# Row shifts of the v tiles: one transfer of 127 or 126 rows, or one of 112 rows and one of the rest

## The chip, the cores and the metric

The kernel runs on one core of one Trainium2 chip. The metric is the device time of one execution in microseconds (us); the figure for a kernel is the median of its timed runs. One further execution was recorded by the hardware profiler. Its record (the trace, and the page of summaries made from it) is where all durations below come from.

Engines are named as in the profile: PE is the matrix engine (PEld its weight loads), DVE the vector engine, ACT the scalar engine, POOL the general-purpose engine, SP the queue processor that issues nearly all transfers here. SPq, DVEq and the like are the sequencers of these engines.

## The reference, cut to what matters

One decoder layer on 256 tokens of width 2048, all in float32. One input projection gives q, k, v, two gate columns per head, a cross-attention query and a SiLU gate path; a gated delta rule works on q, k and v, a cross-attention into 256 memory tokens runs beside it, both are gated and one output projection adds to the residual.

The change touches the causal depthwise convolution that q, k and v pass before the delta rule. Of v there are 3072 columns, and each output row needs its own row and the three rows before it:

```
def causal_depthwise_conv(x, w):          # w has 4 taps
    # y[t, c] = x[t,c] w[3,c] + x[t-1,c] w[2,c] + x[t-2,c] w[1,c] + x[t-3,c] w[0,c]
qkv = silu(causal_depthwise_conv(p[..., :c_qkv], conv_w))
v = qkv[..., 2 * DN_QK_WIDTH:].reshape(B, S, DN_V_HEADS, DN_HEAD_DIM)
```

(The comment line spells out what the library call computes with four taps; rows before the first are zero.)

## The kernel before, in words

**The main stream.** The list `PLAN` (line 55 on) names the weight tiles in the order in which the matrix engine uses them: the memory's values and keys (V, K), the gate columns (ab), the cross-attention query (x), k, q, v and z columns of the input projection, then the output projection (o). One step is one weight tile of 128 x 1024 float32, 512 KB. SP loads it into a staging tile `st` (five buffers); ACT rounds it to the matmul's fp32r format (line 335, the high half of `wt`); DVE subtracts to get the low half (line 339); PE then multiplies high by high, high by low and low by high. `wt` has four buffers, and line 346 keeps two of them prepared ahead. So every weight tile needs a place in the in-order queues of SP, ACT and DVE, and whatever makes one of these engines wait holds up the next weight tile.

`proj_a` (line 355) is used for k and q: the output has the columns on the partitions and the 256 tokens along the free dimension. `proj_b` (line 394) is used for the rest: the output has 128 tokens on the partitions and 512 columns along the free dimension, and there are two such outputs, r = 0 and r = 1, for the two halves of the 256 tokens. The v columns are six proj_b tiles, g = 0 to 5 (`v0` to `v5` in `PLAN`), spread between k, q and z tiles.

**The side work.** Everything that is not the main stream is written as generators. A planned clock, `now[0]`, moves with the planned cost of each matmul; a generator that yields a number is resumed that many planned microseconds later, a plain `yield` resumes it when the operations that it has issued are planned to be over (plus 0.25). `Transfers.dma_start` (line 131, used as `sd`) plans 3.0 us for any transfer, however many it is followed by, and passes it to SP. `VLAND` (line 45) is 5.0, `CALM` 1.6: `calm()` lets a generator wait until DVE's planned queue is short. The program order that results is handed to a framework, which lays out each engine's queue and adds the semaphores.

**The convolution of v** (`v_done`, line 1158). The tokens lie on the partitions, so the value of an earlier token lies on another partition, and a transfer has to move it. For each r, `go()` does this: ACT copies the projection out of PSUM (`vs`); for r = 0 four transfers load the taps (`vw`); `shift(a, val, r, 1)` moves the values down by one row into `a`; five planned microseconds later DVE computes t = v w1 + a w0; `shift(b, two, r, 2)` moves that sum down by two rows into `b`, while DVE computes y = v w3 + a w2; five planned microseconds later DVE adds b. Silu and a scale follow, and with both r done, `delta(g)` (line 1224) does the delta rule for four heads.

`shift(dst, src, r, n)` (line 1162) is therefore called with n = 1 and n = 2 for each of the twelve (g, r). It issues one transfer of 128 - n rows of 2 KB from partitions 0 to 127 - n to partitions n to 127. What is missing at the top, n rows, comes from the last rows of the r = 0 tile when r is 1 (a transfer of n rows), and is zero when r is 0 (a memset on POOL). In the trace the tiles `a`, `b`, `t` and `y` are all called vc, so the shift by one is `vc<-vs` and the shift by two is `vc<-vc`; line 86 is the helper that records every pinned operation and transfer, line 103 the one for DVE, ACT and POOL.

**What else goes through SP around the v tiles.** Weight tiles (`st<-W_d`); rows of the cumulated gate broadcast to all partitions (`erow<-dgc`, line 717), from which ACT computes the decays (`dec`); blocks of the matrix to be inverted, written out and read back (`dN<-dec`, `inN<-dN`, `n<-dN`, `dY<-inXT`, `dX<-inN`, `Y<-dY`, `XN<-dX`, lines 921 to 993).

Of the kernel before, what the change touches and what calls it, by code (L numbers as in the profile page):

```python
# [72 lines left out]
def hybrid_kernel(ctx: ExitStack, tc: tile.TileContext, x, xT, memT, W, prm_d, cst_d, out):  # L73
# [61 lines left out]
    sd = Transfers()  # L135
# [9 lines left out]
    def S2(name, shape, dt=F32):  # L145
        return s2p.tile([128] + list(shape), dt, name=name, tag="s2")
# [26 lines left out]
    def give(pt, t):  # L173

        idle[held.pop(id(pt))[0]].append(t)
# [30 lines left out]
    def spawn(gen, delay=0.0):  # L206
        nproc[0] += 1
        heapq.heappush(heap, (now[0] + delay, nproc[0], gen))
# [21 lines left out]
    def until(cond):  # L230
        while not cond():
            yield POLL
# [14 lines left out]
    def calm(queued=CALM):  # L247

        while ve.end > now[0] + queued:
            yield ve.end - now[0] - queued  # L250
# [907 lines left out]
    def v_done(g):  # L1158

        raw, w, val, two = [None] * 2, [], [None] * 2, [None] * 2  # L1160

        def shift(dst, src, r, n):

            sd.dma_start(dst[n:128], src[r][0 : 128 - n])
            if r:
                sd.dma_start(dst[0:n], src[0][128 - n : 128])
            else:
                po.memset(dst[0:n], 0.0)

        def done(r, pt):  # L1170
            def go():
                yield 0.2
                v = val[r] = S2("vs", [512])
                se.copy(v, pt)
                give(pt, se.end)
                if r == 0:
                    for j in range(4):
                        w.append(S2("vw", [4, 128]))
                        sd.dma_start(w[j], dtap.rearrange("(t k) c -> k t c", k=4)[3 - j][4 * g : 4 * g + 4]
                                     .unsqueeze(0).to_broadcast([128, 4, 128]))  # L1180
                yield
                a, y, t = [S2("vc", [512]) for _ in range(3)]
                shift(a, val, r, 1)
                yield VLAND
                yield from calm()
                w3, w2, w1, w0 = [t_.rearrange("c t e -> c (t e)") for t_ in w]

                ve.tensor_tensor(out=t, in0=v, in1=w1, op=ALU.mult)
                ve.tensor_tensor(out=y, in0=a, in1=w0, op=ALU.mult)
                ve.tensor_tensor(out=t, in0=t, in1=y, op=ALU.add)  # L1190
                two[r] = t
                yield
                yield from until(lambda: two[0] is not None)
                b = S2("vc", [512])
                shift(b, two, r, 2)
                yield from calm()
                ve.tensor_tensor(out=y, in0=v, in1=w3, op=ALU.mult)
                ve.tensor_tensor(out=a, in0=a, in1=w2, op=ALU.mult)
                ve.tensor_tensor(out=y, in0=y, in1=a, op=ALU.add)
                yield VLAND  # L1200
                yield from calm()
                v = y
                ve.tensor_tensor(out=v, in0=y, in1=b, op=ALU.add)
                yield
                se.activation(v, v, AF.Silu)
                vv = v.rearrange("c (w e) -> c w e", w=4)
                yield from until(lambda: all(p in grams for p in (2 * g, 2 * g + 1)))
                for h in range(4):
                    se.activation(vv[:, h, :], vv[:, h, :], AF.Copy, scale=sV[:, r, 4 * g + h : 4 * g + h + 1])
                yield  # L1210
                raw[r] = vv
                ready.add(f"v{g}{r}")
                if r == 1:
                    vss[g] = raw
                    yield from delta(g)
            spawn(go())
        return done
# [271 lines left out]
```

## Time and profile before

| what | value |
|---|---|
| timed runs | 944.04, 945.95, 948.47 us; median 945.95 us |
| the profiled execution | 948.84 us, its span (first to last instruction) 947.1 us |
| PE busy | 868.1 us, 92% of the span |
| DVE busy | 620.4 us, 66% |
| ACT busy | 538.2 us, 57% |
| granted clock of PE, mean over the span | 0.955 |
| transferred | 181.58 MB, 192 GB/s on average |

The page also follows back the chain of work that ended last: at each step to what released it, or to the instruction before it on its engine. An entry "DMA vc<-vs" there is time between the issue of a shift by one and its landing, during which nothing else on that chain was going on; an entry "issue" is time in which an engine waited for something that the profile does not show. A view of waits gives, per engine, the idle time that ended when something else finished, how often, and the longest. A view of windows gives, for stretches of time, the busy time of each engine (with the number of instructions), the granted PE clock as a share of full speed, and the mean busy share of the 16 transfer engines. An engine's idle time costs something only where PE, which is busy nearly throughout, is idle too.

### The profile page before, as it was taken

What the parts mean: (1) busy time and instruction counts of PE and PEld (TensorE: products, weight loads), DVE (VectorE), ACT (ScalarE), POOL (GpSimd) and SP (SyncE); (2) the same over time, 40 slices, a digit from 0 to 9 for tenths busy, and PEclk for the clock granted to TensorE, in tenths of its full rate; (3) what the DMA queues carried; (4) which work ended last, traced back from release to release, by engine and by line L of the source; (5) the groups of instructions that cost most, each with busy time, mean ns of one, the idle gap of its engine ahead of it and who ended that gap; (6) DMA issues with size and microseconds to landing.
All of it is one profiled execution on the core that took longest, in us unless ns stands there. A gap on an engine that the chain in (4) does not pass through costs nothing.

```text
span 947.1 us, 13137 instructions
## 1 busy us (share of the span) xinstructions
PE 868.1 (92%) x4789; PEld 724.3 (76%) x4789; DVE 620.4 (66%) x1080; ACT 538.2 (57%) x927; POOL 44.0 (5%) x45
## 2 busy tenths in 40 slices
PE   8999999999999997967997996965949999999998
PEld 5888888888888876856885884754838888888886
DVE  6769886496799637937777984527558655544442
ACT  6656656887447557825954663645837564343341
POOL 1000000000000000111000001100001000000000
PEclk8999999999999997986998997997979999999999
DMA  9855465477778846646745873645545455856560
GB/s 352 280 186 189 146 217 157 134 211 213 216 246 254 248 133 214 206 156 183 221 141 165 270 214 112 211 134 192 164 126 170 141 178 164 279 190 214 198 214 31
DMA packets 144737, 181.58 MB, mean 192 GB/s; under 512 B 24256, under 2 KB 115256, under 8 KB 144672
## 3 DMA queue, kind: packets, MB, share of 16 engines
q1 hardware_dynamic: 144240, 180.47, 60.4%
q8 instruction: 37, 0.61, 0.3%
q10 hardware_dynamic: 432, 0.28, 0.1%
q14 instruction: 28, 0.23, 0.1%
HBM read 167.58 MB, written 6.89 MB: 184 GB/s over the span
## 4 chain that ended last, share of the span: by engine, by line
PE 76%; DMA 12%; ACT 4%; DVE 3%; issue 2%; SPq 1%; ACTq 0%; DVEq 0%
PE pb L86 63%; DMA vc<-vs 9%; PE pa L86 6%; DMA erow<-dgc 2%; SPq L86 1%; DVE wt L339 1%; PE pU L86 1%; PE pO L86 1%; ACT wt L335 1%; DVE vc L103 1%; PE pm L86 1%; ACT dec L103 1%; PE pyT L86 1%; PE pkq L86 1%; DMA mst<-memT_d 1%
## 5 line engine op out<-in xcount | busy, mean ns | idle before, releaser
L339 DVE TENSOR_TENSOR wt<-st,wt 128x1024 fp32r<-128x1024 f32 (+1 forms) x274 | 332.6, 1217 | 167.7 <-ACT wt L335 165.3
L335 ACT CAST wt<-st 128x1024 fp32r<-128x1024 f32 (+1 forms) x274 | 286.2, 1047 | 245.9 <-PE pb L86 191.7
L86 PE MATMUL pb<-wt,hkt 128*128 128x512 f32 x1536 | 372.0, 400 | 32.6 <-DVE wt L339 32.6
L86 PEld LDWEIGHTS pb<-wt,hkt 128*128 128x128 f32 x1536 | 292.5, 193 | 95.9 <-DVE wt L339 34.8
L86 PE MATMUL pb<-wt,yhi 128*128 128x512 f32 x512 | 158.0, 390 | 0.0
L86 PE MATMUL pa<-hkt,wt 128*128 128x512 f32 (+1 forms) x768 | 144.5, 345 | 8.0 <-ACT raw L103 7.7
L86 PEld LDWEIGHTS pa<-hkt,wt 128*128 128x128 f32 x768 | 119.9, 192 | 26.1 <-ACT raw L103 8.0
L86 PEld LDWEIGHTS pb<-wt,yhi 128*128 128x128 f32 x512 | 95.7, 188 | 19.6
L86 PE MATMUL pb<-wt,ylo 128*128 128x512 f32 x256 | 99.7, 389 | 0.0
L86 PE MATMUL pb<-wt,mkt 128*128 128x512 f32 x384 | 92.2, 400 | 2.7 <-DVE mkt L103 1.9
L86 PEld LDWEIGHTS pb<-wt,mkt 128*128 128x128 f32 x384 | 73.6, 193 | 20.1 <-issue 3.2
L103 DVE TENSOR_TENSOR vc<-vc,vw 128x512 f32<-128x512 f32 x24 | 16.5, 687 | 77.0 <-DMA vc<-vs 60.5
L86 PEld LDWEIGHTS pb<-wt,ylo 128*128 128x128 f32 x256 | 48.1, 188 | 10.1
L103 ACT ACT_TABLE_LOAD x31 | 39.8, 1283 | 4.1 <-DVE acc L103 3.6
L103 ACT ACTIVATE acc<-raw,prm 128x256 f32<-128x256 f32 x24 | 12.1, 505 | 46.1 <-DVE raw L103 46.1
L103 DVE SCALAR_TENSOR_TENSOR acc<-raw,prm,acc 128x255 f32<-128x255 f32 (+2 forms) x72 | 34.3, 477 | 2.5 <-ACT acc L103 2.1
L103 DVE TENSOR_TENSOR inT<-inXT,inN 96x1 f32<-96x1 f32 (+22 forms) x92 | 29.2, 343 | 3.3 <-DMA inN<-dN 2.5
L103 DVE TENSOR_REDUCE inXT<-inT 96x1 f32<-96x1 f32 (+22 forms) x92 | 28.6, 338 | 0.7
L86 PE MATMUL pO<-u,aT 128*128 128x128 f32 x96 | 13.7, 288 | 15.5 <-ACT u L103 15.5
L86 PEld LDWEIGHTS pO<-u,aT 128*128 128x128 f32 x96 | 12.8, 203 | 16.2 <-ACT u L103 15.9
L103 DVE TENSOR_TENSOR vc<-vc 128x512 f32<-128x512 f32 x36 | 24.6, 684 | 0.1
L103 ACT ACTIVATE dec<-erow,gcc 128x128 f32<-128x128 f32 x48 | 16.1, 392 | 13.8 <-DMA erow<-dgc 13.8
(202 smaller groups left out, 697.2 us busy)
## 6 DMA issues: line engine op xcount, KB each, us to landing
st<-W_d SPq DMA_DIRECT2D x272, 512.0 KB
erow<-dgc SPq DMA_DIRECT2D x24, 256.0 KB
vw<-dtap SPq DMA_DIRECT2D x24, 256.0 KB
dN<-dec SPq DMA_DIRECT2D x12, 256.0 KB
n<-dN SPq DMA_DIRECT2D x12, 256.0 KB
vc<-vs SPq DMA_DIRECT2D x12, 254.0 KB
vc<-vc SPq DMA_DIRECT2D x12, 252.0 KB
xraw<-xT_d SPq DMA_DIRECT2D x8, 256.0 KB
```

Source lines behind the costliest of these rows:

```text
L86: return lambda *a, **k: pin(getattr(self.eng, op)(*a, **k))
L103: return pin(getattr(self.eng, op)(*a, **k))
L335: pin(se.eng.copy(hi[:, w] if parts > 1 else hi, st[:, w] if parts > 1 else src))
L339: pin(ve.eng.tensor_tensor(out=lo[:, w] if parts > 1 else lo, in0=st[:, w] if parts > 1 else src, in1=hi[:, w] if parts > 1 else hi, op=AL ...
```

## The change

The transfer of 128 - n rows in `shift` becomes two: rows 0 to 111 (112 rows) go to partitions n to 111 + n, and the remaining 16 - n rows (15 for n = 1, 14 for n = 2) go to partitions 112 + n to 127. The same bytes land in the same places. The transfer or memset of the top n rows is untouched, and so are the pauses, the order in which the work is written down and everything else. Over the kernel, 24 transfers become 48.

```
         def shift(dst, src, r, n):
 
-            sd.dma_start(dst[n:128], src[r][0 : 128 - n])
+
+            sd.dma_start(dst[n : 112 + n], src[r][0:112])
+            sd.dma_start(dst[112 + n : 128], src[r][112 : 128 - n])
             if r:
                 sd.dma_start(dst[0:n], src[0][128 - n : 128])
             else:
```

## The prediction

> **What bounds the kernel now.** I read first where PE has idle time, in a table of three stretches of the span (length, then busy time and instruction count of PE, PEld, DVE, ACT, POOL, then PE clock, transfer share, GB/s):
>
> ```profile
> 0.00:340.00 340.00, 335.77 (x1883) 278.90 (x1884) 257.14 (x484) 217.18 (x347) 17.32 (x23) 0.99 0.69 217
> 340.00:720.00 380.00, 309.07 (x1853) 258.93 (x1852) 245.93 (x455) 220.35 (x430) 20.07 (x19) 0.90 0.57 176
> 720.00:947.10 227.10, 223.22 (x1057) 186.48 (x1055) 117.29 (x143) 100.63 (x150) 6.64 (x3) 1.00 0.55 180
> ```
>
> PE is idle for 380.00 - 309.07 = 70.9 us between 340 and 720, and for only 4.2 and 3.9 us in the stretches before and after. Between 340 and 720 the clock is also granted at 0.90 only. This is the stretch in which the six v tiles are convolved. Next I asked PE what ended each of its waits there (us in total, times, longest):
>
> ```profile
> PE pb L86 <- DVE wt L339: 32.6, 4, 17.0
> PE pO L86 <- ACT u L103: 15.5, 1, 15.5
> PE pyT L86 <- DVE kcl L103: 13.0, 1, 13.0
> PE pa L86 <- ACT raw L103: 7.7, 1, 7.7
> PE pm L86 <- issue: 1.1, 2, 0.8
> PE pm L86 <- DMA Y<-dY: 1.0, 1, 1.0
> ```
>
> Four rows, seven waits, make 32.6 + 15.5 + 13.0 + 7.7 = 68.8 us. They name DVE and ACT, but neither is overworked; they were late themselves. So the third view is what ended DVE's own waits, and the fourth the chain of work that ended last (start, length, what), around each PE wait:
>
> ```profile
> DVE vc L103 <- DMA vc<-vs: 60.5, 9, 10.3
> DVE vc L103 <- issue: 16.5, 1, 16.5
> ```
>
> ```profile
> 342.82 6.84 SPq L86
> 349.71 10.18 DMA erow<-dgc
> ...
> 404.85 13.95 DMA vc<-vs
> 418.79 10.30 issue
> 429.10 0.76 DVE vc L103 x2
> ...
> 491.18 18.67 DMA vc<-vs
> ...
> 566.27 18.70 DMA vc<-vs
> ...
> 627.60 17.88 DMA vc<-vs
> ...
> 682.54 17.72 DMA vc<-vs
> ```
>
> Each v tile has one such piece, and five of the six name the shift by one, 13.95 to 18.70 us from issue to landing. DVE then stands in front of the product that reads `a`, in order, with the subtraction for the next weight tile queued behind it: that is how PE comes to wait for `wt`. The 16.5 us row has no named releaser; it lies in v1 and ends in a vc product. SP's time line there shows three issues, the shift of r = 0, the one-row copy and the shift of r = 1, over 6.19 us:
>
> ```profile
> 404.85 6.19 SPq L86 DMA_DIRECT2D vc<-vs  x3
> ```
>
> So the second shift went out about 5.5 us after the first and landed later still; I read the 16.5 us as the wait for it. At v0 the chain shows something else that I read as the same cause: SP held for 6.84 us in issuing, and a broadcast of 256 KB that took 10.18 us. Undisturbed, the same kind takes less than half:
>
> ```profile
> 174.64 4.24 DMA erow<-dgc
> ```
>
> **Why these transfers and not the others.** The group table of the page has both kinds of shift, and the issue table their sizes:
>
> ```profile
> L103 DVE TENSOR_TENSOR vc<-vc,vw 128x512 f32<-128x512 f32 x24 | 16.5, 687 | 77.0 <-DMA vc<-vs 60.5
> L103 DVE TENSOR_TENSOR vc<-vc 128x512 f32<-128x512 f32 x36 | 24.6, 684 | 0.1
> vc<-vs SPq DMA_DIRECT2D x12, 254.0 KB
> vc<-vc SPq DMA_DIRECT2D x12, 252.0 KB
> ```
>
> The readers of the shift by one (127 rows, 254 KB) stood idle for 77.0 us. The sums and the readers of the shift by two (126 rows, 252 KB) stood idle for 0.1 us, with the same five planned microseconds between issue and use. Nearly the same bytes, the same memory, the same queue: what differs is 127 against 126. 127 has no divisor but itself, 126 = 14 x 9 has; 112 = 16 x 7. A transfer that is dealt out in equal shares can then not be shared at 127 rows, but can at 126 and at 112. And whatever else has a share on the one engine that holds 254 KB waits behind it, which fits the late broadcast at v0. The page on DMA of the Trainium skill ("DMA: Bandwidth & Descriptors", section "Why a DMA increments its semaphore by 16 and not by 1") states this as a rule: a transfer uses the largest number of engines up to 16 that divides the slowest dimension of both sides, so 127 partitions run on one. By that rule 126 rows run on 14, 112 on 16, 15 on 15 and 14 on 14, and the two rows above agree, though neither shows the number of engines.
>
> **The change, part by part.** *Removed: the long landing of the twelve shifts by one.* The row nearest in size to a 112-row transfer (224 KB) that is shared is the 4.24 us broadcast; the next is a read-back in the same stretch, the longer end:
>
> ```profile
> 590.31 5.40 DMA Y<-dY
> ```
>
> The lower end is that it lands within the five planned us whatever it takes. So the new landing lies between "covered" and 5.40 us; I take 4.24, the nearer in size, covered by the pause of 5. The work that hides it is the main stream, which the planner put into those five us. If that cover is gone (DVE ahead of plan), the price is up to 4.24 us a time. With it the 68.8 us of PE waits go: all seven end, through DVE's or ACT's queue, in the shift or in what stood behind it. The two small pm rows, 2.1 us, I leave in: they belong to the matrix inverse. What is late next is PE itself.
>
> *Removed with it: the slow clock after each wait.* The stretches after the waits:
>
> ```profile
> 361.32:380.00 18.68, 18.59 (x85) 15.60 (x86) 18.46 (x32) 17.88 (x32) 0.00 (x0) 0.86 0.67 207
> 432.40:445.00 12.60, 12.60 (x44) 10.75 (x45) 10.04 (x17) 7.74 (x23) 0.19 (x3) 0.63 0.89 239
> 513.20:520.00 6.80, 6.79 (x22) 5.48 (x23) 6.80 (x11) 6.77 (x15) 2.04 (x1) 0.73 0.48 129
> 588.40:600.00 11.60, 10.63 (x39) 8.09 (x39) 10.07 (x22) 5.13 (x11) 6.23 (x2) 0.85 0.69 157
> 649.10:660.00 10.90, 10.90 (x43) 9.03 (x44) 10.90 (x19) 7.71 (x14) 0.00 (x0) 0.80 0.84 265
> 703.30:720.00 16.70, 16.70 (x80) 14.60 (x81) 16.67 (x28) 10.35 (x21) 0.00 (x0) 0.86 0.51 151
> ```
>
> The time lost is length times (1 - clock): 18.68 x 0.14 = 2.6, 12.60 x 0.37 = 4.7, 6.80 x 0.27 = 1.8, 11.60 x 0.15 = 1.7, 10.90 x 0.20 = 2.2, 16.70 x 0.14 = 2.3; together 15.3 us. That is the upper end, since DVE is as full as PE in four of the six, catching up; the lower end is half of it, 7.7. I take the upper end, because DVE's backlog goes with the same wait.
>
> *Added: 24 more issues on SP, and 24 more landings to wait for.* What an issue costs SP stands in the view of the tile vc (shortest, median, longest, in ns):
>
> ```profile
> L86 SPq DMA_DIRECT2D vc<-vs x18: 600/2184/10082, 333.8 to 682.5; - x18
> L86 SPq DMA_DIRECT2D vc<-vc x18: 631/817/4303, 362.4 to 703.7; - x18
> SPq L86 <- DVE wt L339: 101.8, 40, 6.4
> ```
>
> The third row is from SP's waits between 340 and 720. An unhindered issue takes 0.63 to 0.82 us, so 24 of them 15.1 to 19.7 us of SP. Behind them in SP's queue stand the weight loads. SP waits 101.8 us in that stretch for a staging buffer to come free, so it has room for 20 us; with five buffers, a load 0.8 us later is not felt. The cost at the end lies between 0 (below nothing too: the 10.08 us issue, held behind earlier transfers, should shrink) and 12 x 0.82 = 9.8 us, if each extra issue of a shift by one lay on the path to DVE. I take 4 us, the middle a little towards the cover. For the shifts by two, whose readers waited 0.1 us, splitting brings nothing and costs the issue alone, counted here.
>
> **Sum.** 947.1 - 68.8 - 15.3 + 4 = 867.0 us of span. The profiled execution took 948.84 us, 1.74 more than its span, so 868.7; the median of the runs, 945.95, lies 2.9 below it, so 865.8: **866 us**. As a check, 380 - 84.1 + 4 leaves 300 us for 245.93 us of DVE, 82%. The kernel does more than that elsewhere with PE full:
>
> ```profile
> 260.00:320.00 60.00, 60.00 (x290) 50.43 (x289) 55.40 (x112) 37.76 (x53) 0.00 (x0) 1.00 0.81 240
> ```
>
> DVE at 55.40 of 60 and PE at 60.00 of 60.
>
> **The rivals.** *DVE becomes the bound of the v stretch.* It goes in order and is fed by chains with landings in them; over the first 340 us it ran at 257.14 / 340 = 0.756. If it can't be packed closer than that, its 245.93 us need 325 us in place of 380: a gain of 55, and 945.95 - 55 = 891 us. For it: DVE is as full as PE in four of the six stretches after a wait. Against it: the row of 260 to 320 above. 0.17.
>
> *No change.* The 127-row transfers are slow for another reason that 112 rows share (the odd start partition, or the crowd of transfers around them). Then the landing stays at 14 to 18 us and the time at 946, give or take 4. For it: no row shows 112 rows. Against it: the shifts by two start off the same grid, in the same stretch, and nobody waits for them. 0.04.
>
> *Slower: the parts only add.* The two parts run one behind the other on the same path, land no earlier than one did, and each issue is one more for SP, on which the weight loads wait. The price is the SP time of 24 issues at 0.63 us or more, 15 us: 961 us. It decides if SP's issues, and not the landing, hold DVE; the 15 us then lie on the path that already ends the waits. For it: SP was held for up to 10.08 us in one issue. Against it: those long issues are for this very kind of transfer, and the shift by two, also issued by SP, has a median of 0.82. The Trainium skill's page on DMA, section "Rules for kernel authors", speaks for this rival: two transfers to disjoint partition ranges are not worth making, as they go over the same engines one after the other, and its section on SWDGE gives about 2.0 us of fixed cost for a transfer, an estimate of 48 us for 24. No run here shows that price. 0.04.
>
> **How the numbers follow.** The forecast has 0.75, because 127 against 126 rows is as clean a comparison as a trace offers. Its own range: down to 858 (no added cost, the 2.1 us of pm gone as well, and the 1.9 us by which the lowest run lies under the median), up to 883 (clock gain halved, 7.7; added cost 9.8 in place of 4; and the profile's 2.9 not taken off). The range takes in the rival of DVE with 5 us about it: 857 to 896. Left out are the two other rivals, 0.08, and some 0.1 of the first two beyond the ends. A measurement of this kernel can tell about 0.5%, 4.7 us, from no change. Faster by more than that 0.92, within it 0.04, slower 0.04.
>
> **What would show it right or wrong.** Right: the vc product that reads `a` has no waits for a shift longer than 2 us, the chain has no "DMA vc<-vs" piece over 6 us, the broadcast near 350 lands in about 4 us, SP's longest issue of a shift is under 3 us, and PE's idle time between the first and the last v tile is under 10 us at a clock of 0.98 or more. Wrong: the 112-row part still takes over 10 us; or its landing is short and PE waits as long as before for `wt`, behind DVE that is busy (first rival) or behind SP (third). A span near 867 with the clock still at 0.90 would mean that two terms of the sum were off in opposite ways.

## The result and the profile after

The changed kernel takes 861.52 us (median of four runs, 859.21 to 861.90) against 947.21 us for the kernel before (median of four runs, one more than above): a ratio of 0.9095, 95% interval 0.9064 to 0.9125. The profiled execution took 861.81 us, its span is 860.0 us, and the granted clock is 1.0 on average, 0.955 before. One of the four executions of cut_113, further down, ran at a granted clock of 0.651 and took 1233.64 us; it is left out of that kernel's figures.

The three stretches again; the middle one, with the v tiles, is 80 us shorter, so it ends at 640 (length, then busy time and count of PE, PEld, DVE, ACT, POOL, then clock, transfer share, GB/s):

```profile
0.00:340.00 340.00, 337.23 (x1890) 279.94 (x1891) 257.11 (x484) 218.03 (x348) 17.33 (x23) 1.00 0.69 218
340.00:640.00 300.00, 298.18 (x1884) 250.96 (x1883) 249.88 (x464) 225.56 (x443) 25.87 (x20) 1.00 0.74 228
640.00:860.00 220.00, 216.26 (x1019) 180.53 (x1017) 112.33 (x133) 95.09 (x138) 3.27 (x2) 1.00 0.54 178
```

PE's idle time in the middle went from 70.9 to 1.8 us, at a clock of 1.00 in place of 0.90. All of PE's waits that are left, over the whole span:

```profile
PE pb L86 <- DVE wt L339: 2.0, 4, 1.1
PE warm L86 <- DVE warm L103: 1.2, 1, 1.2
PE pb L86 <- DVE mkt L103: 0.7, 1, 0.7
PE pa L86 <- DVE wt L339: 0.3, 1, 0.3
```

Two of these rows are the start of the kernel. What other engines still wait for on account of transfers of these kinds:

```profile
ACT dec L103 <- DMA erow<-dgc: 3.9, 4, 1.7
DVE vc L103 <- DMA vc<-vs: 2.7, 1, 2.7
...
ACT wt L335 <- DMA st<-W_d: 0.7, 2, 0.5
```

Of the kernel before, beside the 60.5 us for the shift that the prediction shows:

```profile
ACT wt L335 <- DMA st<-W_d: 20.7, 7, 9.2
ACT dec L103 <- DMA erow<-dgc: 16.0, 6, 11.8
```

So it is not only the reader of the shift that is served sooner. The weight tiles and the broadcasts, which the change doesn't touch, are too: 20.7 to 0.7 us and 16.0 to 3.9 us. The chain of work that ended last holds these transfers (start, length):

```profile
1.65 5.46 DMA mst<-memT_d
...
173.37 4.24 DMA erow<-dgc
...
399.14 5.66 DMA vc<-vs
...
567.76 5.86 DMA vc<-vs
```

Two pieces of 5.66 and 5.86 us are left of the five of 13.95 to 18.70; both begin with the issue of a 15-row part. SP's issues of the shifts (shortest, median, longest in ns; the top rows count among them):

```profile
L86 SPq DMA_DIRECT2D vc<-vs x30: 545/634/1910, 332.5 to 607.9; - x30
L86 SPq DMA_DIRECT2D vc<-vc x30: 528/640/1691, 351.5 to 617.8; - x30
```

There are 60 in place of 36, but the longest is 1.91 us where it was 10.08.

### The profile page after: what moved, and what is told of

It reads as the page before. It is cut to its first block, busy times and chain, and to the rows that moved or that the text cites. A ratio compares the mean times of both kernels' runs of the same rounds, so it can differ in the third digit from the quotient of the medians.

```text
span 860.0 us, 13169 instructions
## 1 busy us (share of the span) xinstructions
PE 851.7 (99%) x4789; PEld 711.4 (83%) x4789; DVE 619.3 (72%) x1080; ACT 538.7 (63%) x927; POOL 46.5 (5%) x45
## 4 chain that ended last, share of the span: by engine, by line
PE 89%; DVE 3%; ACT 3%; DMA 2%; issue 1%; SPq 0%; ACTq 0%; DVEq 0%
PE pb L86 69%; PE pa L86 11%; PE pO L86 2%; PE pU L86 2%; DMA vc<-vs 1%; DVE wt L339 1%; PE pm L86 1%; DVE vc L103 1%; PE pkq L86 1%; PE pyT L86 1%; ACT dec L103 1%; DMA mst<-memT_d 1%; PE pqs L86 1%; DVE acc L103 1%; PE pkk L86 1%
## 5 line engine op out<-in xcount | busy, mean ns | idle before, releaser
L86 PE MATMUL pb<-wt,hkt 128*128 128x512 f32 x1536 | 362.3, 393 | 1.5 <-DVE wt L339 1.5
L86 PEld LDWEIGHTS pb<-wt,hkt 128*128 128x128 f32 x1536 | 284.6, 188 | 60.7 <-DVE wt L339 2.5
L86 PE MATMUL pa<-hkt,wt 128*128 128x512 f32 (+1 forms) x768 | 142.7, 341 | 0.4 <-DVE wt L339 0.3
L86 PEld LDWEIGHTS pa<-hkt,wt 128*128 128x128 f32 x768 | 117.8, 188 | 18.2 <-DVE wt L339 1.0
L86 PEld LDWEIGHTS pb<-wt,ylo 128*128 128x128 f32 x256 | 48.1, 188 | 10.1
L103 POOL TENSOR_TENSOR e<-e,mhalf 128x8 f32<-128x8 f32 x6 | 20.8, 3474 | 120.3 <-DVE e L103 120.3
L103 POOL TENSOR_TENSOR srk<-skt,mhalf 128x4 f32<-128x4 f32 x6 | 7.1, 1176 | 224.7 <-DVE skt L103 224.7
L103 DVE SCALAR_TENSOR_TENSOR o<-o,e,zs 128x128 f32<-128x128 f32 x48 | 14.0, 344 | 7.0 <-POOL e L103 7.0
L103 ACT ACTIVATE ojunk<-o 128x128 f32<-128x128 f32 x48 | 14.4, 301 | 5.7 <-DVE o L103 3.7
```

Source lines behind the costliest of these rows:

```text
L86: return lambda *a, **k: pin(getattr(self.eng, op)(*a, **k))
L103: return pin(getattr(self.eng, op)(*a, **k))
```

## The experiments

My theory, called the sharing theory in the expectations: a transfer is dealt out in equal shares over the largest number of engines up to 16 that divides its rows, so 127 rows go over one engine, and what is queued on that engine waits with them. The rivals: smaller transfers help as such; another order in the engines' queues (the framework lays the queues out anew when a transfer is added) made the gain; SP held in issuing was the trouble; the wait of the shift's reader is all that costs. Twelve kernels were made to tell these apart. In the edits, `m` is the row at which the shift is cut: rows 0 to m - 1 in one transfer, the rest, if any, in another.

**Which of the two shifts.**

```
-            sd.dma_start(dst[n : 112 + n], src[r][0:112])
-            sd.dma_start(dst[112 + n : 128], src[r][112 : 128 - n])
+            m = 112 if n == 1 else 126      # split_one;   split_two: m = 127 if n == 1 else 112
+            sd.dma_start(dst[n : m + n], src[r][0:m])
+            if m + n < 128:
+                sd.dma_start(dst[m + n : 128], src[r][m : 128 - n])
```

> Only the shift by one is split (112 + 15 rows); the shift by two goes as one transfer of 126 rows, as before. Sharing theory (a transfer is dealt out over the largest number of engines up to 16 that divides its rows; 127 rows sit on one): the whole gain is here, 858 to 866 us, PE idle time under 8 us. Rival (smaller transfers help as such, both shifts alike): the shift by two gives its part back, 870 us or more.

> Only the shift by two is split (112 + 14 rows); the shift by one goes as one transfer of 127 rows. Sharing theory: nothing is gained, 940 to 950 us, and DVE's products that read the shift by one wait for it as before, some 60 us. Rival (smaller transfers help as such, or another order of the queues made the gain): 905 us or less.

Splitting the shift by one alone gives 861.63 us, ratio 0.911 (0.9095 to 0.9125): the whole gain. Splitting the shift by two alone gives 944.65 us, 0.9995 (0.9977 to 1.0014): none, with the same number of added transfers. In the latter DVE waits for the shift as it did before, where it was 60.5 us in nine waits and 16.5 us in one without a named releaser, 77.0 us in ten:

```profile
DVE vc L103 <- DMA vc<-vs: 75.9, 10, 17.0
```

Here all ten name the shift, which supports the prediction's reading of the 16.5 us row. Cutting up a transfer of 126 rows is worth nothing, and twelve more issues cost nothing that can be seen.

**Where the cut falls.** The same edit with other values of `m` for n = 1. In cut_113, cut_122 and cut_124 (the shift by two cut at 112, as in the changed kernel) every engine's queue holds the same instructions in the same order as the changed kernel; only the row counts of the two parts differ. In cut_126 the shift by two is whole, as in split_one.

> The shift by one is split one row later: 113 + 14 rows. Every engine's queue holds the same instructions in the same order as in the changed kernel, only the sizes of these two transfers differ by a row. 113 has no divisor. Sharing theory: the 113 rows sit on one engine, 113/127 of the long landing, 12 to 17 us, and nearly the whole loss returns: 925 to 945 us. Rival (order of the queues, or two smaller transfers): as the changed kernel, 858 to 866 us.

> The shift by one is split as 122 + 5 rows, queues again in the same order as in the changed kernel. 122 = 2 x 61. Sharing theory: two engines with 61 rows each, about half of the long landing, 7 to 10 us, of which the planned pause covers 5: some 870 to 900 us, between the changed kernel and the cut at 113. Rival (any even count is as good as 112): 858 to 866 us. Rival (only a count that gives all 16 engines helps): 925 us or more.

> The shift by one is split as 124 + 3 rows, every queue in the same order as in the changed kernel. 124 = 4 x 31. Sharing theory: four engines with 31 rows each, half of the 61 rows of the cut at 122, which took 887.7 us; the landing should be near the five planned microseconds: 862 to 872 us. Rival (only counts that give nearly all engines help): 885 us or more.

> The shift by one is split as 126 + 1 rows, the shift by two not split. Sharing theory: 126 = 14 x 9 rows go over 14 engines, the one row is dealt out as 16 pieces like the one-row copy that is there already: as the changed kernel, 858 to 866 us. Rival (the cut must fall on a multiple of 16, or the parts be clearly smaller than the whole): 900 us or more, since 126 rows are 99% of the bytes.

| kernel | larger part of the shift by one | median, us | ratio to before, interval |
|---|---|---|---|
| cut_113 | 113 rows, no divisor | 929.12 | 0.9822 (0.9795 to 0.9850) |
| cut_122 | 122 = 2 x 61 | 887.73 | 0.9386 (0.9372 to 0.9401) |
| cut_124 | 124 = 4 x 31 | 868.80 | 0.9177 (0.9159 to 0.9195) |
| cut_126 | 126 = 14 x 9 | 861.03 | 0.9096 (0.9074 to 0.9118) |
| the change | 112 = 16 x 7 | 861.52 | 0.9095 (0.9064 to 0.9125) |

All four fell within what the sharing theory expected. A single row moved from one part to the other, 112 to 113, costs 68 us, with no instruction added, removed or put elsewhere: the order of the queues did not make the gain. And 126 rows, nearly all the bytes, do as well as 112. What counts is the largest divisor up to 16, and the time falls with the rows per engine, 113, 61, 31, 9; between 9 and 7 no difference can be told. The waits of DVE for the shift, kernel by kernel, cut_113 first, then cut_122, then cut_124:

```profile
DVE vc L103 <- DMA vc<-vs: 62.0, 10, 13.1
```

```profile
DVE vc L103 <- DMA vc<-vs: 23.6, 7, 6.0
```

```profile
DVE vc L103 <- DMA vc<-vs: 8.9, 5, 2.9
```

And the shifts in the chain that ended last, of cut_113 and of cut_124:

```profile
409.28 16.91 DMA vc<-vs
...
489.27 10.59 DMA vc<-vs
...
557.46 16.22 DMA vc<-vs
623.76 9.11 DMA vc<-vs
674.45 8.96 DMA vc<-vs
```

```profile
395.60 7.42 DMA vc<-vs
...
574.73 7.86 DMA vc<-vs
613.29 8.73 DMA vc<-vs
```

A piece is named after the tile, and can be any transfer of the shift. In cut_113 the first piece is the 113-row part and the third the 14-row part; in cut_124 the first is the 124-row part. The others are the one-row copy from the r = 0 tile.

The traces also hold every update of a transfer's semaphore, the counter by which a transfer tells that it has landed. From these records, for the twelve transfers of each kind (issue to last update, in us):

| kernel | transfer | updates of its semaphore, each | landing: shortest, median, longest |
|---|---|---|---|
| before | 127 rows | 2 | 13.3, 15.9, 23.6 |
| before, shift by two | 126 rows | 15 | 3.1, 3.9, 10.8 |
| cut_113 | 113 rows | 2 | 11.9, 14.1, 18.7 |
| cut_122 | 122 rows | 3 | 8.6, 9.2, 13.2 |
| cut_124 | 124 rows | 5 | 6.9, 7.6, 10.9 |
| cut_126 | 126 rows | 15 | 3.1, 5.8, 7.0 |
| the change | 112 rows | 16 | 2.6, 5.9, 7.8 |

The sharing theory gives these transfers 1, 14, 1, 2, 4, 14 and 16 engines. The updates are that number, and one more wherever it is under 16. In tail_127, described next, the one more is an update 1.1 us after the issue, before the first row moves; the other comes 12.8 us after it, when the last row has moved. The smaller parts fit as well: 15 updates for 14 rows, 6 for 5 rows, 4 for 3 rows.

In the changed kernel the product that reads `a` starts 6.3 to 12.5 us after the 112-row part is issued. That is the cover there is in fact. Landings of up to 7.8 us fit into it but for one wait of 2.7 us; with four engines, up to 10.9 us, DVE waits 8.9 us and the kernel is 7 us slower.

**The transfer alone.** One transfer more, of `m` rows, at the very end of the changed kernel, when the last result has been computed and nothing else is to run:

```
                     sy.dma_start(out[...], res[r][:, w])
+                if cb == 3 and r == 1:
+                    sd.dma_start(S2("tail", [512])[1 : m + 1], res[r][0:m])
```

> The changed kernel with one more transfer at the very end, when nothing else is left to run: 127 rows of the last result tile, one partition down, into a tile that nobody reads; the output is the same. The span then ends with its landing, so its price can be read alone. Sharing theory: one engine moves 127 rows at 0.08 to 0.11 us each, 10 to 14 us, so 8 to 13 us longer than with 112 rows. Rival (the transfer is only slow among others): within 2 us of 112 rows.

> The same with 126 rows. Sharing theory: 14 engines, 9 rows each, within 1 us of 112 rows. Rival (size, or the odd start partition): as 127 rows.

> The same with 112 rows, the control. Both theories: 1 to 3 us longer than the changed kernel.

The medians are 870.64, 862.73 and 862.07 us (ratios 0.9195, 0.9111, 0.9102; each interval is within 0.002 of it). 127 rows cost 8.6 us more than 112, 126 rows cost 0.7, less than a measurement can tell. The control cost less than expected, 0.5 us over the changed kernel: in its trace the last result lands 1.5 us after the issue of the extra transfer, and the extra transfer 2.6 us after it. The issues, on the time line of each, in the order 127, 126, 112:

```profile
855.03 0.68 SPq L86 DMA_DIRECT2D tail<-res  x1
```

```profile
855.86 0.88 SPq L86 DMA_DIRECT2D tail<-res  x1
```

```profile
858.75 0.58 SPq L86 DMA_DIRECT2D tail<-res  x1
```

The spans end at 868.6, 859.8 and 862.2 us. So 127 rows need 13.6 us from the issue to the end, 126 rows 3.9, and 112 rows 3.5. Hardly anything else moves then (the last result's rows are through 0.9 us after the issue), so the slowness is the transfer's own. In the trace the 127 rows follow one another over 11.1 us, at most two in flight at a time; the 112 rows take 1.1 us. One engine has 127 rows in place of 7, and 10.1 us for 120 more rows is 0.084 us for a row of 2 KB, which is also the median that the trace records for one row.

**Who pays: the reader, or whatever is queued behind.** A transfer of 127 rows that nobody reads, and a control of 112 rows with every queue in the same order:

```
+    spill = [dp.tile([128, 512], F32, name=f"spill{i}", tag=f"spill{i}") for i in range(12)]
 ...
                 shift(a, val, r, 1)
+                sd.dma_start(spill[2 * g + r][0:127], v[0:127])      # unread_112: 112
```

> The changed kernel, and behind each shift by one a further transfer, issued by SP, of 127 rows of vs to a scratch in memory that nobody reads (twelve in all); it computes the same. Crowding part of the sharing theory: the 127 rows sit on one engine and hold up whatever has a share there, the second half's shift, the broadcasts, the weight tiles: 880 to 930 us against the 112-row control, and PE waits of 15 to 60 us. Rival (only the wait of the shift's own reader costs): within 6 us of the control.

> The control of the run before: the same extra transfer with 112 rows, every queue in the same order. Both theories: 858 to 872 us, since 12 shared transfers of 224 KB and 12 issues are a small addition.

The control takes 868.32 us, ratio 0.9161 (0.9135 to 0.9187); with 127 rows it is 939.72 us, 0.9921 (0.9898 to 0.9944). Twelve transfers that no instruction waits for cost 71 us, more than I expected, and most of the 86 us that the change saved on the twelve that were read. ACT's and DVE's waits with the 127 rows:

```profile
ACT wt L335 <- DMA st<-W_d: 65.1, 10, 16.3
DVE vc L103 <- DMA vc<-vs: 34.7, 6, 8.4
ACT dec L103 <- DMA erow<-dgc: 14.7, 4, 9.4
```

and the weight tiles in the chain that ended last, which there take about as long as the shifts did before:

```profile
422.36 10.45 DMA st<-W_d
...
490.42 18.25 DMA st<-W_d
...
631.20 17.17 DMA st<-W_d
```

In the control the first of these waits is

```profile
ACT wt L335 <- DMA st<-W_d: 6.3, 6, 2.3
```

The semaphore of every weight tile is updated 16 times in these traces: it has a share on every engine, and is there only when its last share is. Crowding alone is therefore enough to make a loss of this size, without any reader that waits for the slow transfer.

**Another queue.** As the kernel before, but the shift by one issued by ACT:

```
-            sd.dma_start(dst[n:128], src[r][0 : 128 - n])
+            if n == 1:
+                nc.scalar.dma_start(dst[1:128], src[r][0:127])
+            else:
+                sd.dma_start(dst[2:128], src[r][0:126])
```

> As before, 127 and 126 rows in one transfer each, but the shift by one is issued from ACT's queue in place of SP's. Sharing theory: the rows still sit on one engine, DVE still waits some 50 to 75 us for the shift, and what else has a share on that engine still waits behind it: 920 to 950 us. Rival (what hurt was that SP stood held in issuing, up to 10.08 us, with the weight loads behind it): 880 us or less.

974.93 us, 1.0301 (1.0268 to 1.0334): slower than before, outside what either theory expected. SP is no longer held in issuing shifts, its longest such issue is 1.44 us, and it brought nothing. But the holding has only moved to ACT (shortest, median, longest in ns):

```profile
L1166 ACTq DMA_DIRECT2D vc<-vs x12: 608/3164/7335, 340.9 to 701.1; - x12
```

DVE's two rows and one of SP's:

```profile
DVE vc L103 <- DMA vc<-vs: 73.5, 9, 10.0
DVE vc L103 <- issue: 27.7, 2, 22.6
```

```profile
SPq L86 <- DMA vc<-vs: 50.8, 5, 13.2
```

The last row is new: SP itself now waits for shifts to land. In each of the five waits the transfer that SP issues next counts on the same semaphore as the shift that it waited for. Both may add to the time, so the run shows that another issuing queue is not the remedy, but not how much the holding cost by itself; that stays open. Five of the chain's pieces "DMA vc<-vs" are 26.58 to 29.61 us long here, each the second 127-row transfer of a pair; why they are longer than before was not tried.

## Why the prediction was right, step by step

*The cause* was read rightly: 127 rows against 126, and sharing by divisors. cut_113 shows it with queues that are otherwise equal, tail_127 with hardly any traffic around. The rule for the number of engines in the Trainium skill ("DMA: Bandwidth & Descriptors", "Why a DMA increments its semaphore by 16 and not by 1") agrees with the times and with the semaphore updates of every count that was tried, 113, 122, 124, 126, 127 and 112 rows. The comparison of the two shifts in the trace before was less clean than I called it: three more products of DVE, some 2 us, stand between the issue of the shift by two and its use. The cut experiments don't rest on it.

*A misreading that changed no number:* of the five chain pieces that I took for the long shift, three (491.18, 627.60, 682.54) are the one-row copy, issued last. So is the issue of 10.08 us, which I counted as one of a 127-row transfer against the third rival; the longest of those is 5.05 us. The copy of 2 KB lands 12.8 to 18.7 us after its issue, with 16 updates, and 1.7 to 6.6 us after it in the changed kernel. That is the crowd behind a single engine, already in the trace before.

*The PE waits, 68.8 us:* 69.1 came (70.9 before, 1.8 left). That the two small pm rows would stay was wrong. They are gone, and 1.5 us of two new short waits for `wt` stand in their place.

*The slow clock, 15.3 us:* PE's busy time over the two later stretches fell from 309.07 + 223.22 to 298.18 + 216.26, by 17.8 us. Of that 1.3 us is work that lies before 340 now, because the start went faster in this execution (the broadcast at 174.64 stands at 173.37, ahead of anything that was changed). That leaves 16.6 us, the upper end and a little more; my six stretches left out a short one near 578.

*The added cost, 4 us:* nothing of it can be seen. I take the 24 issues to be hidden in SP's waits for staging buffers, as forecast; no run took these waits away. The changed kernel with 24 lies at 861.52 us, split_one and cut_126 with 12 at 861.63 and 861.03.

*The sum:* 867.0 us of span was forecast, 860.0 came. The 7.0 us are 4 (added cost), 1.3 (clock), 1.3 (start), 0.3 (waits) and 0.1 (the end). *The landing of 4.24 us* was too short for the traffic of that stretch: the twelve 112-row parts land after 2.6 to 7.8 us, median 5.9, eight of them beyond my longer end of 5.40. The cover still held, but not for the reason that I gave, five planned microseconds: it was 6.3 to 12.5 us in fact, and that was luck. DVE waited once, for 2.7 us, not under the 2 us that I had set as a sign, and the broadcast near 350, now at 342.96, takes 5.2 us and not about 4; the other signs came as set.

*The rivals.* DVE did not become the bound: 249.88 us of work in 300 is 0.83, above the 0.756 of that rival, with PE busy for 298.18. "No change" and "the parts only add" fall with the result itself. The 2.0 us per transfer that I took for the latter from the Trainium skill ("DMA: Bandwidth & Descriptors", "Anatomy of one DMA — SWDGE (gpsimd) path") stands there for transfers issued by the general-purpose engine, and all here are issued by SP or ACT; no run shows such a price, and 24 more transfers for the same bytes cost nothing that can be seen. The advice of the Trainium skill ("DMA: Bandwidth & Descriptors", "Rules for kernel authors") against two transfers to disjoint partition ranges agrees with split_two, where the whole was already shared; it does not hold where the cut changes the number of engines, as split_one shows with 0.911. What I had underrated is the crowd: I named the late broadcast as one effect, and the unread transfers show that the queue behind a single engine can by itself cost 71 us, where the change gained 86.

## What to carry to other kernels

Look at the row count of every transfer on the path. A shift by one of a full tile has 127 rows, which share with nothing; cut off one row or fifteen, so that the larger part has a divisor near 16. And look for such transfers also where nobody waits for them: if weight tiles land late now and then, ask what stood on one engine ahead of them.

## What the runs showed of the hardware that I had not expected

Twelve unread transfers of 127 rows cost 71 us; the largest wait that they made is for weight tiles, 65.1 us against 6.3 us in the control, up to 16.3 us at a time. The number of engines can be read from a trace: a transfer of 127 rows updates its semaphore twice, one of 126 rows 15 times, one of 112 rows 16 times. And the price of sharing is steep at the low end only: one engine 929.12 us, two 887.73, four 868.80, fourteen 861.03; between fourteen and sixteen there was nothing to measure.
